# The prompt's down projection of a SwiGLU FFN as seven block products for eight, with the sample's part behind it

## The chip, the cores and the metric

The kernel runs on one core of a Trainium2 chip. The time is the device time of one execution in microseconds (us); three runs of the kernel before are at hand, and one more execution with a profile. Engines: TensorE (PE in the profile; its weight loads are PEld), VectorE (DVE), ScalarE (ACT), GpSimd (POOL) and SyncE (SP), which issues most of the transfers.

## The reference

One encoder layer and a final norm, applied to a prompt (1024 tokens) and a sample (256 tokens) with the same weights; D_MODEL is 1024 and D_FF 2816. The parts ahead of the FFN are left out here.

```python
    h = rmsnorm(x, norm_ffn_w)
    gu = h @ ffn_w_gate_up
    x = x + (jax.nn.silu(gu[..., :D_FF]) * gu[..., D_FF:]) @ ffn_w_down
    return x
...
        return rmsnorm(x, final_norm_w)
```

## The kernel before

Activations lie with channels on the 128 partitions and tokens along the free axis. Tokens are three blocks (`BLOCKS`): two of 512 for the prompt and one of 256 for the sample. D_FF is 22 tiles f of 128, D_MODEL 8 tiles m (or k) of 128. Matrices are fp32, and each operand is split into a rounded part and its remainder (`split`: ACT copies it to fp32r, L125; DVE or POOL subtracts, L126). `mm3` (L108) makes one product of three matmuls: hi by hi, hi by lo, lo by hi.

PE runs its instructions in the order in which the program writes them. The other engines are ordered by a tile scheduler, which works with estimates of durations and the dependences; each engine, and each queue of transfers, then runs its list strictly in order. Work to be done beside the main products (the norms) is written as side generators that yield a number of ns to wait for (`LAGS`, `LAGF`, `PACEF`), and `K.main` puts their PE instructions between the products when they are due by its own clock.

The up projection (`ff_first` for f = 0, `ff_up` for f = 1 to 21) already makes the prompt's gate and up of one f by seven block products for eight. Its outputs per f are the gated values of the prompt's two blocks and of the sample. Before, they go to DRAM as they are (`gd`, one row per f; `times_up`).

The down projection (`ffn_down`, `down`) reads them back. It goes over eight groups of f (`DOWN`: 2, 2, then six of 3). Within a group it goes over 8 m and 3 blocks; a PSUM bank sums a group's f, and DVE adds 0.5 times the bank to the residual in SBUF (L1717). So 192 banks are read. Weights of a group (`in_w_dn`, one tile of 128 x 1024 per f) are split on ACT and DVE, the gated values (`g_load`, 128 x 1280) on ACT and POOL or DVE. In the last group a `Norm` per block adds up squares as each m is done (`nm.add`, by POOL for the first `FADD[b]` of them, else DVE). Its rest (`Norm.rest`) sums them over partitions on PE (`nacc`), takes a reciprocal root on DVE (`nst`, ten small operations, L224 to L228), spreads it over partitions on PE, and scales and stores the output. The sample's norm is the last of all, behind the last product.

In front of the up projection stands the norm of the third block's FFN input. It is a side generator with the lag `LAGS`, so its PE instructions fall between products of the first f. Four banks hold raw operands (`r2_raw`) there, until L1535 has read them.

Of the kernel before, what the change touches and what calls it, by code (L numbers as in the profile page):

```python
# [8 lines left out]
F32 = mybir.dt.float32  # L9
# [20 lines left out]
DOWN = ((0, 1), (2, 3)) + tuple((f, f + 1, f + 2) for f in range(4, NFF, 3))  # L30
# [133 lines left out]
def trunk_kernel(ctx: ExitStack, tc: tile.TileContext, a):  # L164
# [1236 lines left out]
    gd = dp.tile([NFF, P, NTOK], F32, name="gd")  # L1401
# [136 lines left out]
    def make_room():  # L1538
        nonlocal room, c22
        room = x0p.tile([P, KT, 512], F32, tag="x0", name="room")  # L1540
        c22 = room[:, 7, :]

    fp = room = c22 = None
# [8 lines left out]
    def copied(ps, t=None):  # L1552
        if t is None:
            turns["p"] += 1
            t = room[:, 4 + turns["p"] % 3, :]
# [16 lines left out]
    def gate_of(ps, p, g=None):  # L1572
        g = ff(x2p, "nacc", "g", bufs=2) if g is None else g
        V.tensor_tensor(out=g, in0=p, in1=ps, op=ALU.add)  # L1574
        return silu2(g)

    def times_up(t, u, f, t0, n, sign):
        V.scalar_tensor_tensor(out=t, in0=u, scalar=sign, in1=t, op0=ALU.mult, op1=ALU.mult)
        SY.dma_start(gd[f, :, t0 : t0 + n], t)

    K.lo_vector = True
    K.order += [(a["w_dn"][g], "fp" if g > 1 and g % 3 else "wp") for g in range(NFF)]
    g_of = {}

    def g_load(i):

        if i == len(DOWN):
            return
        gh, gl = (hp.tile([P, 3, NTOK], F32R, tag=f"{x}{i % 2}", name=f"g{x}") for x in ("hi", "lo"))
        g_of[i] = []  # L1590
        for j, f in enumerate(DOWN[i]):
            for sl in (slice(0, 640), slice(640, NTOK)) if i == 0 else (slice(0, NTOK),):
                raw = K.raw()[:, :640] if i == 0 else fp.tile([P, NTOK], F32, tag="graw", name="graw", bufs=3)
                SY.dma_start(raw, gd[f, :, sl])
                split(gh[:, j, sl], gl[:, j, sl], raw, V if j % 2 else G)
            g_of[i].append((gh[:, j, :], gl[:, j, :]))
# [7 lines left out]
    def ff_first():  # L1604
# [19 lines left out]
        t2 = gate_of(pf, u2, u2)  # L1624
# [12 lines left out]
        u3 = copied(pa, cs[:, 2, :])  # L1637
        V.tensor_tensor(out=u3, in0=u3, in1=pe, op=ALU.add)
        times_up(t2, u3, 0, 512, 512, -1.0)
        yield from gu_mm(pa, w(3), 1, t4, False)  # L1640
        times_up(t1, pa, 0, 0, 512, -1.0)

    def ff_up(f):
# [198 lines left out]
```

## Time and profile before

| | us |
|---|---|
| median of three runs (lowest, highest) | 2325.65 (2325.51, 2326.88) |
| the profiled execution, its own time | 2328.12 |
| its span, first to last instruction | 2326.3 |

| | |
|---|---|
| mean granted clock | 0.989 |
| first down product starts | 1995.54 us |
| last down product starts | 2310.83 us |

A page gives the busy time per engine, the span in 40 slices with tenths of busy time, the granted clock in tenths and GB/s, the queues, the chain that ended last, the costliest groups and the transfers with the time from issue to landing. Rows of the trace give start, duration, engine, line, operation, output and inputs by the program's names, partitions by elements, and in brackets the idle time ahead of it and what ended that.

### The profile page before, as it was taken

To read this page: it belongs to the slowest core of one execution; us is meant where nothing else is said; L and a number is where in the kernel's file an instruction comes from. 1 tells how busy PE (TensorE), PEld (TensorE's weight loads), DVE (VectorE), ACT (ScalarE), POOL (GpSimd) and SP (SyncE) were. 2 spreads that over 40 slices of the span, in tenths; PEclk is the share of its full clock that TensorE was granted. 3 is DMA by queue.
4 is the path that set the end of the run, shared out by engine and by line. 5 is a ranking of instruction groups with operands and counts; after the bars stand their busy time and mean duration, and the time that the engine had idled before them with its cause. 6 is when DMAs were issued, how large, how long until landed. Compare 5 with 4: busy or idle time off the path is not lost.

```text
span 2326.3 us, 32511 instructions
## 1 busy us (share of the span) xinstructions
PE 2241.6 (96%) x12596; PEld 1947.7 (84%) x12596; DVE 1313.0 (56%) x2759; ACT 754.1 (32%) x1387; POOL 567.6 (24%) x362
## 2 busy tenths in 40 slices
PE   6999999999999999999999998999999999999997
PEld 6988888888888888888888886888888888888886
DVE  7758687887976955554543557323223223656445
ACT  5433242333423433132344523322322322312113
POOL 3010000000000000021322420766566565212113
PEclk9999999999999999999999999999999999999998
DMA  5221412323243537861223422211211211723202
GB/s 182 87 86 50 116 49 84 83 59 91 71 122 107 181 104 242 261 209 68 91 87 108 160 73 73 86 62 64 73 62 64 91 62 52 260 87 112 73 10 91
DMA packets 170453, 237.84 MB, mean 102 GB/s; under 512 B 71530, under 2 KB 99002, under 8 KB 170298
## 3 DMA queue, kind: packets, MB, share of 16 engines
q1 hardware_dynamic: 150458, 206.65, 28.0%
q10 hardware_dynamic: 19840, 29.11, 3.4%
q8 instruction: 99, 1.62, 0.3%
q14 instruction: 56, 0.46, 0.1%
HBM read 166.20 MB, written 69.51 MB: 101 GB/s over the span
## 4 chain that ended last, share of the span: by engine, by line
PE 46%; DVE 2%; DMA 1%; issue 1%; POOL 1%; ACT 0%; POOLq 0%; ACTq 0%; DVEq 0%; SPq 0%
PE bank L108 45%; DMA raw<-in_w_dn 0%; DMA kraw<-vd 0%; PE bank L121 0%; POOL x L272 0%; POOL wlo L126 0%; DVE wlo L126 0%; POOL kv L126 0%; DMA kraw<-kd 0%; DMA raw<-in_w_gu 0%; DVE x L1717 0%; DMA raw<-gd 0%; DVE t4l L126 0%; DVE x L1526 0%; DVE r2l L126 0%
## 5 line engine op out<-in xcount | busy, mean ns | idle before, releaser
L108 PE MATMUL bank<-hi,whi 128*128 128x512 f32 (+1 forms) x2144 | 766.5, 358 | 0.9 <-ACT whi L125 0.9
L108 PE MATMUL bank<-hi,wlo 128*128 128x512 f32 (+1 forms) x2144 | 751.1, 350 | 2.9 <-POOL wlo L126 1.8
L108 PE MATMUL bank<-lo,whi 128*128 128x512 f32 (+1 forms) x2144 | 751.4, 350 | 0.4 <-POOL lo L126 0.4
L108 PEld LDWEIGHTS bank<-hi,wlo 128*128 128x128 f32 x2144 | 407.2, 190 | 58.1 <-POOL wlo L126 2.2
L108 PEld LDWEIGHTS bank<-hi,whi 128*128 128x128 f32 x2144 | 408.1, 190 | 51.2 <-ACT whi L125 1.4
L108 PEld LDWEIGHTS bank<-lo,whi 128*128 128x128 f32 x2144 | 408.2, 190 | 49.9 <-POOL lo L126 0.7
L126 POOL TENSOR_TENSOR wlo<-raw,whi 128x1024 fp32r<-128x1024 f32 x71 | 180.5, 2545 | 439.1 <-ACT whi L125 435.9
L125 ACT ACTIVATE whi<-raw 128x1024 fp32r<-128x1024 f32 x151 | 159.4, 1060 | 355.5 <-PE bank L108 281.5
L108 PE MATMUL bank<-ghi,whi 128*128 128x512 f32 (+1 forms) x528 | 189.3, 358 | 1.3 <-DVE x L1717 1.3
L108 PE MATMUL bank<-ghi,wlo 128*128 128x512 f32 (+1 forms) x528 | 188.3, 357 | 0.5 <-DVE wlo L126 0.5
L108 PE MATMUL bank<-glo,whi 128*128 128x512 f32 (+1 forms) x528 | 187.3, 355 | 0.0
L1717 DVE SCALAR_TENSOR_TENSOR x<-bank,x 128x512 f32<-128x512 f32 (+1 forms) x192 | 112.4, 598 | 125.3 <-PE bank L108 120.0
L126 POOL TENSOR_TENSOR wlo<-room,whi 128x1024 fp32r<-128x1024 f32 x42 | 100.8, 2400 | 129.5 <-ACT whi L125 129.5
L126 DVE TENSOR_TENSOR wlo<-raw,whi 128x1024 fp32r<-128x1024 f32 x80 | 106.6, 1338 | 31.0 <-ACT whi L125 30.9
L108 PEld LDWEIGHTS bank<-ghi,whi 128*128 128x128 f32 x528 | 99.3, 188 | 17.2 <-DVE x L1717 2.2
L108 PEld LDWEIGHTS bank<-ghi,wlo 128*128 128x128 f32 x528 | 99.2, 188 | 16.4 <-DVE wlo L126 1.0
L108 PEld LDWEIGHTS bank<-glo,whi 128*128 128x128 f32 x528 | 99.4, 188 | 15.1
L126 POOL TENSOR_TENSOR glo<-graw,ghi 128x1280 fp32r<-128x1280 f32 x13 | 46.3, 3576 | 203.7 <-ACT ghi L125 203.7
L1680 DVE TENSOR_TENSOR room<-room,bank 128x512 f32<-128x512 f32 x21 | 14.4, 687 | 143.2 <-ACT room L1556 143.2
L125 ACT ACTIVATE whi<-room 128x1024 fp32r<-128x1024 f32 x42 | 44.5, 1061 | 143.4 <-PE bank L108 143.4
L1574 DVE TENSOR_TENSOR g<-room,bank 128x512 f32<-128x512 f32 x42 | 28.9, 688 | 103.4 <-PE bank L108 103.4
L591 DVE SCALAR_TENSOR_TENSOR acc<-craw,sm,acc 128x510 f32<-128x510 f32 (+1 forms) x96 | 72.5, 756 | 25.4 <-ACT acc L589 24.3
(302 smaller groups left out, 3803.2 us busy)
## 6 DMA issues: line engine op xcount, KB each, us to landing
raw<-in_w_gu SPq DMA_DIRECT2D x44, 512.0 KB, 3.9
graw<-gd SPq DMA_DIRECT2D x20, 640.0 KB, 5.5
gd<-t SPq DMA_DIRECT2D x44, 256.0 KB, 2.5
raw<-in_w_dn SPq DMA_DIRECT2D x22, 512.0 KB, 4.3
raw<-in_w_g SPq DMA_DIRECT2D x20, 512.0 KB, 3.5
gtd<-gs ACTq DMA_DIRECT2D x32, 256.0 KB, 2.0
raw<-in_w_qkv SPq DMA_DIRECT2D x12, 512.0 KB, 3.6
x<-in_xT SPq DMA_DIRECT2D x10, 512.0 KB, 5.7
```

The source lines that it names most:

```text
L108: self.nc.tensor.matmul(out, l, r, start=start, stop=stop, skip_group_check=more)
L125: self.nc.scalar.activation(hi, src, AF.Copy)
L126: (eng or self.nc.vector).tensor_tensor(out=lo, in0=src, in1=f32(hi), op=ALU.subtract)
L591: V.scalar_tensor_tensor(out=dst, in0=src, scalar=wj, in1=dst, op0=ALU.mult, op1=ALU.add)
L1574: V.tensor_tensor(out=g, in0=p, in1=ps, op=ALU.add)
L1680: V.tensor_tensor(out=c22, in0=u3, in1=pe, op=ALU.add)
L1717: V.scalar_tensor_tensor(out=x2[b][:, m, :], in0=ps, scalar=0.5, in1=x2[b][:, m, :], op0=ALU.mult, op1=ALU.add)
```

## The change

The prompt's down projection is written as seven block products over pairs of f: a pair (even f, odd f) by the two halves of D_MODEL is one side, by the two blocks of tokens the other. The second operand (B) is combined in `combine` as the gated values are made, and seven versions are stored for each of 11 pairs (`gq`); the sample's go to `gsd`. The first operand (A, weights) is combined on DVE in `a_prep`. A phase is one of the seven products: 11 pairs by 4 tiles of 128 output channels, summed in four banks ("a" or "b") over all pairs; "b" and "a" are kept over several phases, and 28 evictions of 512 wide take the place of 128. Within a phase, weights come in units of one or two pairs (`a_split` into a ring of three) and B in bundles of 3, 4 and 4 pairs (`b_load`, `b_split`). The first units and bundles are loaded in the last f of the up projection (`down_early`). The sample's part (`down_sample`) follows, with f one after the other, and 8 evictions. The norm of block 1 starts after the sixth phase, that of block 0 after the seventh, that of the sample at the end. `nm.add` for the prompt is on POOL, for the sample on DVE. `LAGS` and the second `LAGF` grow.

```diff
-DOWN = ((0, 1), (2, 3)) + tuple((f, f + 1, f + 2) for f in range(4, NFF, 3))
+PAIRS = NFF // 2
...
-    gd = dp.tile([NFF, P, NTOK], F32, name="gd")
+    gq = dp.tile([7, PAIRS, P, 512], F32, name="gq")
+    gsd = dp.tile([NFF, P, NS], F32, name="gsd")
...
+    def combine(f, t1, t2):
+        p = f // 2
+        if f % 2 == 0:
+            r = ff(x2p, "nacc", "r", bufs=2)
+            V.tensor_tensor(out=r, in0=t1, in1=t2, op=ALU.subtract)
+            SY.dma_start(gq[2, p], r)
+            pending["r"], pending["b12"] = r, t2
             return
+        r, b12 = pending["r"], pending["b12"]
+        V.scalar_tensor_tensor(out=r, in0=r, scalar=-1.0, in1=t2, op0=ALU.mult, op1=ALU.subtract)
+        SY.dma_start(gq[3, p], r)
+        V.tensor_tensor(out=b12, in0=t2, in1=b12, op=ALU.subtract)
+        SY.dma_start(gq[4, p], b12)
+        t4_ = ff(x2p, "nsq", "t", bufs=3) if f == NFF - 1 else t1
+        V.scalar_tensor_tensor(out=t4_, in0=r, scalar=-1.0, in1=t1, op0=ALU.mult, op1=ALU.subtract)
+        SY.dma_start(gq[6, p], t4_)
+    def store1(f):
+        return gq[f % 2, f // 2]
+    def store2(f):
+        return gq[5, f // 2] if f % 2 else None
...
+    units = [slice(0, 1)] + [slice(i, i + 2) for i in range(1, PAIRS, 2)]
+    bundles = [slice(0, 3), slice(3, 7), slice(7, PAIRS)]
+    unit_of = {p: i for i, u in enumerate(units) for p in range(u.start, u.stop)}
+    bundle_of = {p: i for i, u in enumerate(bundles) for p in range(u.start, u.stop)}
+    w_dn = a["w_dn"].rearrange("(k e) p m -> e p k m", e=2)
...
+    def b_load(j):
+        if j >= 7 * len(bundles):
+            return
+        ph, i = divmod(j, len(bundles))
+        ps = bundles[i]
+        n = ps.stop - ps.start
+        if j == 0:
+            raw = x2p.tile([P, 4, 512], F32, tag="x2", name="braw")
+        else:
+            raw = hp.tile([P, 4, 512], F32, tag="lo2" if j % 2 and j > 1 else "hi2", name="braw")
+        SY.dma_start(raw[:, :n, :], gq[ph, ps].rearrange("k p t -> p k t"))
+        b_raw[j] = raw
+    def b_split(j):
+        if j >= 7 * len(bundles):
+            return
+        ps = bundles[j % len(bundles)]
+        t = hp.tile([P, 2, 4, 512], F32R, tag="lo0" if j % 2 else "hi0", name="bhl")
+        n = ps.stop - ps.start
+        raw = b_raw.pop(j)
+        for x in ([0, 1] if n == 3 else [0, 2]):
+            sl = slice(x, x + 1 if n == 3 and x == 0 else x + 2)
+            split(t[:, 0, sl, :], t[:, 1, sl, :], raw[:, sl, :], V)
+        b_hl[j] = t
+    def a_room(i):
+        if i % 3 < 2:
+            return tuple(t.rearrange("p (k c) -> p k c", c=512) for t in pair_of(wp))
+        t = down_room()
+        return t[:, 0], t[:, 1]
+    def a_split(i, src):
+        n = src.shape[1]
+        a_hl[i] = tuple(t[:, :n, :] for t in a_room(i))
+        split(*a_hl[i], src, V)
...
+    def down_early(step):
+        if step == 0:
+            b_load(0)
+            early_raw(1, K.raw()[:, :1024].rearrange("p (k c) -> p k c", c=512))
+            pair_home(0)
+            SY.dma_start(home[0][0][0], w_dn[0][:, units[0], :])
+            b_split(0)
+            a_split(0, part(0, 0, 0))
+        elif step == 1:
+            b_load(1)
+            t = hp.tile([P, 4, 512], F32, tag="lo2", name="araw")
+            early_raw(2, t[:, 0:2, :])
+            early_raw(3, t[:, 2:4, :])
+        else:
+            a_split(1, early[1])
+            b_split(1)
+            b_load(2)
...
+            combine(*pending["last"])
...
+    def down_room():
+        return dpool.tile([P, 2, 2, 512], F32R, tag="x2", name="ahl")
...
+    def a_prep(i):
+        ph, u = divmod(i, len(units))
...
+        if ph == 0:
+            src = early[u] if u in early else p(0, 0)
+        elif ph == 1:
+            src = p(1, 0)
+        elif ph == 2:
+            src = p(0, 1)
+            V.tensor_tensor(out=src, in0=src, in1=p(1, 1), op=ALU.add)
...
+        else:
+            src = p(1, 1)
+        a_split(i, src)
+    STEPS = (("a", 0, 0, 0, 1), ("b", 0, 0, 0, 1), ("b", 0, 1, 1, -1), ("a", 1, 0, 1, 1), ("a", 1, 1, 1, -1), ("b", 1, 0, 1, 1), ("a", 1, 1, 0, -1))
...
+    def down_prompt():
+        a_prep(2)
+        norms = {}
+        for b in (1, 0):
+            norms[b] = Norm(x2p, 512)
+        sums = {}
+        for ph, (key, more, half, b, sign) in enumerate(STEPS):
+            if not more:
+                sums[key] = [bank(pm if key == "a" else pq) for _ in range(4)]
+            ps = sums[key]
+            def product(m, p, start, stop):
+                i = len(units) * ph + unit_of[p]
+                j = len(bundles) * ph + bundle_of[p]
+                k, q = p - units[unit_of[p]].start, p - bundles[bundle_of[p]].start
+                t = b_hl[j]
+                x = [(*(w[:, k, m * P : (m + 1) * P] for w in a_hl[i]), t[:, 0, q, :], t[:, 1, q, :])]
+                yield from mm3(ps[m], x, start and not more, stop, bool(more))
+            final = (half, b) in ((0, 0), (1, 1), (0, 1), (1, 0)) and ph in (1, 4, 5, 6)
+            def evac(m):
+                x = x2[b][:, 4 * half + m, :]
+                V.scalar_tensor_tensor(out=x, in0=ps[m], scalar=0.5 * sign, in1=x, op0=ALU.mult, op1=ALU.add)
+                if final:
+                    norms[b].add(x, G)
+            for u, pairs in enumerate(units):
+                i = len(units) * ph + u
+                pairs = range(pairs.start, pairs.stop)
+                if u < len(units) - 1:
+                    for p in pairs:
+                        for m in range(4):
+                            yield from product(m, p, p == 0, False)
+                else:
+                    for m in range(4):
+                        for p in pairs:
+                            yield from product(m, p, False, p == PAIRS - 1)
+                        evac(m)
+                for load in loads.get(i, ()):
+                    load[0](*load[1:])
+                if i == 1:
+                    pair_home(1)
+                    SY.dma_start(home[1][0][0], w_dn[1][:, units[0], :])
+                a_prep(i + 3)
+                if pairs[-1] + 1 == bundles[bundle_of[pairs[-1]]].stop:
+                    j = len(bundles) * ph + bundle_of[pairs[-1]]
+                    b_split(j + 2)
+                    if j == 0:
+                        b_load(3)
+                    b_load(j + 4)
+                if ph == 6:
+                    sample_loads(u)
+            if ph == 5:
+                last_norm(norms[1], 1)
+        last_norm(norms[0], 0)
...
+    order_s = [2 * p + 1 for p in range(PAIRS)] + [2 * p for p in range(PAIRS)]
+    g_s = {}
+    def g_room(i, tag, n):
+        t = hp.tile([P, 2, n, NS], F32R, tag=tag, name="gs")
+        for k in range(i, min(i + n, NFF), 2):
+            raw = x2p.tile([P, 512], F32, tag="nsq", name="graw", bufs=3).rearrange("p (k t) -> p k t", k=2)
+            for x in range(2):
+                SY.dma_start(raw[:, x, :], gsd[order_s[k + x]])
...
+    def down_sample():
+        for us in ((0,), (1, 2), (3, 4), (5,)):
+            w_load(0, 0, us)
+        g_room(16, "hi0", 6)
+        nm = Norm(x2p, NS)
+        his, los = ([t[:, 512 * k : 512 * k + 512] for t in (w0, w1) for k in range(2)] for w0, w1 in zip(pair_of(wp), pair_of(wp)))
+        def prep(n):
+            if n < 2 * NFF:
+                half, i = divmod(n, NFF)
+                e, p = (1, i) if i < PAIRS else (0, i - PAIRS)
+                t, k = home[e][unit_of[p]]
+                k += p - units[unit_of[p]].start
+                split(his[n % 4], los[n % 4], t[:, k, 512 * half : 512 * half + 512], V)
+        for n in range(4):
+            prep(n)
+        for half in range(2):
+            ps = [bank(pm)[:, :NS] for _ in range(4)]
+            def product(m, i):
+                n = NFF * half + i
+                sl = slice(m * P, (m + 1) * P)
+                yield from mm3(ps[m], [(his[n % 4][:, sl], los[n % 4][:, sl], *g_s[i])], i == 0, i == NFF - 1)
+            for i in range(NFF - 2):
+                for m in range(4):
+                    yield from product(m, i)
+                prep(NFF * half + i + 4)
+                if half == 0 and i == 2:
+                    for us in ((0,), (1, 2), (3, 4), (5,)):
+                        w_load(0, 1, us)
+            for m in range(4):
+                for i in range(NFF - 2, NFF):
+                    yield from product(m, i)
+                x = x2[2][:, 4 * half + m, :]
+                V.scalar_tensor_tensor(out=x, in0=ps[m], scalar=0.5, in1=x, op0=ALU.mult, op1=ALU.add)
+                nm.add(x, V)
+            for i in range(NFF - 2, NFF):
+                prep(NFF * half + i + 4)
+        last_norm(nm, 2)
...
-            nm = Norm(x2p, n)
-            for m in range(KT):
-                yield from down(g_of[i], ws, m, b)
-                nm.add(x2[b][:, m, :], G if m < FADD[b] else V)
...
-LAGS, FIRST_W = 13500, 9000
+LAGS, FIRST_W = 19000, 9000
-LAG0, LAGF, PACEF = 7500, (3500, 2800, 1500), 500
-FADD = (6, 4, 0)
+LAG0, LAGF, PACEF = 7500, (3500, 3500, 1500), 500
```

PE in the first f of the up projection: `hi`, `lo`, `hi1`, `lo1` are the parts of the activations, `whi`, `wlo` those of a weight, `cst` by `nacc` is the norm's sum over partitions. Before:

```order
L108 MATMUL bank_13393<-hi1_12890,wlo_13379 128x512 [waits DVE_49]
L108 MATMUL bank_13393<-hi1_12890,whi_13378 128x512 [waits Activation_49]
L108 MATMUL bank_13393<-lo1_12891,whi_13378 128x512
L108 MATMUL bank_13393<-hi1_12890,wlo_13379 128x512
L108 MATMUL bank_13459<-cst_74,nacc_12587 128x1 [waits DVE_49,PE_49]
L108 MATMUL bank_13459<-cst_74,nacc_12587 128x1
L108 MATMUL bank_13393<-hi1_12890,whi_13378 128x512 [waits Activation_49]
L108 MATMUL bank_13393<-lo1_12891,whi_13378 128x512
L108 MATMUL bank_13393<-hi1_12890,wlo_13379 128x512
L108 MATMUL bank_13393<-hi1_12890,whi_13378 128x512 [waits Activation_49]
```

After:

```order
L108 MATMUL bank_13509<-hi0_12889,whi_13465 128x512
L108 MATMUL bank_13509<-lo0_12890,whi_13465 128x512
L108 MATMUL bank_13509<-hi0_12889,wlo_13466 128x512
L108 MATMUL bank_13509<-hi0_12889,whi_13465 128x512
L108 MATMUL bank_13509<-lo0_12890,whi_13465 128x512
L108 MATMUL bank_13509<-hi0_12889,wlo_13466 128x512
L108 MATMUL bank_13519<-cst_74,nacc_12588 128x1 [waits DVE_49,PE_49]
L108 MATMUL bank_13519<-cst_74,nacc_12588 128x1
L108 MATMUL bank_13509<-hi0_12889,whi_13465 128x512
L108 MATMUL bank_13509<-lo0_12890,whi_13465 128x512
L108 MATMUL bank_13509<-hi0_12889,wlo_13466 128x512
```

The norm's sum stood inside the product of the third weight, behind one that reads tile `hi1`; it stands inside a later-written product of `hi0` now, with the bank of `r2_raw` no longer next.

ACT where the up projection ends and the down projection begins: `bhl` is a split bundle, `ahl` and `whi` a split unit, `braw` and `araw` what was loaded for them. Before:

```order
L125 ACTIVATE whi_17484<-raw_17482 128x1024 [waits DMAHW4_49,Pool_49]
L1556 ACTIVATE room_13526<-bank_17313 128x512 [waits PE_49,Activation_49]
L125 ACTIVATE whi_17490<-raw_17488 128x1024 [waits DMAHW5_49,Pool_49]
L1568 ACTIVATE t_17508<-g_17506 128x512 [waits DMAHW1_49,DVE_49]
L125 ACTIVATE whi_17558<-raw_17532 128x1024 [waits DMAHW6_49,PE_49]
L125 ACTIVATE ghi_17568<-graw_17570 128x1280 [waits DMAHW1_49,PE_49]
L125 ACTIVATE ghi_17568<-graw_17574 128x1280 [waits DMAHW2_49]
L125 ACTIVATE whi_17772<-raw_17746 128x1024 [waits DVE_49,DMAHW3_49,Activation_49,Pool_49]
L125 ACTIVATE whi_17564<-raw_17562 128x1024 [waits DMAHW7_49,PE_49]
```

After:

```order
L1557 ACTIVATE room_13508<-bank_17352 128x512 [waits DMAHW0_49,PE_49]
L1569 ACTIVATE t_17549<-room_13508 128x512 [waits DMAHW6_49,DVE_49]
L125 ACTIVATE bhl_17529<-braw_17506 128x1024 [waits DMAHW4_49]
L125 ACTIVATE bhl_17529<-braw_17506 128x1024
L125 ACTIVATE whi_17602<-araw_17508 128x1024 [waits DMAHW5_49,PE_49,Activation_49]
L125 ACTIVATE bhl_17638<-braw_17534 128x1024 [waits DMAHW0_49,PE_49]
L125 ACTIVATE bhl_17638<-braw_17534 128x1024
L125 ACTIVATE ahl_17581<-araw_17508 128x1024 [waits DMAHW4_49,DMAHW3_49,DMAHW6_49,DMAHW2_49,DVE_49]
L125 ACTIVATE whi_17634<-w0_17573 128x1024 [waits DMAHW6_49,Activation_49]
L125 ACTIVATE ahl_17673<-w0_17575 128x1024 [waits DMAHW7_49,DVE_49,PE_49]
```

Splits of a weight and of gated values stood by turns; now the split of unit 2 (`ahl_17581`, of `araw_17508`) stands behind that of unit 3 (`whi_17602`) and that of the third bundle (`bhl_17638`), which waits for PE and for the transfer into `braw_17534`.

DVE in the norm of block 1: `nst` is its reciprocal root, `bank` a scratch row. Before:

```order
L227 TENSOR_TENSOR bank_19592<-bank_19592,nst_19597 128x4 [waits DVE_49]
L228 SCALAR_TENSOR_TENSOR nst_19597<-bank_19592,nst_19597 128x4 [waits DVE_49]
L226 SCALAR_TENSOR_TENSOR bank_19592<-nst_19597,bank_19592 128x4 [waits DVE_49]
L1717 SCALAR_TENSOR_TENSOR x1_17524<-bank_19588,x1_17524 128x512 [waits PE_49]
L227 TENSOR_TENSOR bank_19592<-bank_19592,nst_19597 128x4 [waits DVE_49]
L228 SCALAR_TENSOR_TENSOR nst_19597<-bank_19592,nst_19597 128x4 [waits DVE_49]
L226 SCALAR_TENSOR_TENSOR bank_19592<-nst_19597,bank_19592 128x4 [waits DVE_49]
L227 TENSOR_TENSOR bank_19592<-bank_19592,nst_19597 128x4 [waits DVE_49]
L228 SCALAR_TENSOR_TENSOR nst_19597<-bank_19592,nst_19597 128x4 [waits DVE_49]
L1717 SCALAR_TENSOR_TENSOR x1_17524<-bank_19619,x1_17524 128x512 [waits PE_49]
```

After:

```order
L228 SCALAR_TENSOR_TENSOR nst_18775<-bank_18770,nst_18775 128x4 [waits DVE_49]
L226 SCALAR_TENSOR_TENSOR bank_18770<-nst_18775,bank_18770 128x4 [waits DVE_49]
L227 TENSOR_TENSOR bank_18770<-bank_18770,nst_18775 128x4 [waits DVE_49]
L228 SCALAR_TENSOR_TENSOR nst_18775<-bank_18770,nst_18775 128x4 [waits DVE_49]
L226 SCALAR_TENSOR_TENSOR bank_18770<-nst_18775,bank_18770 128x4 [waits DVE_49]
L227 TENSOR_TENSOR bank_18770<-bank_18770,nst_18775 128x4 [waits DVE_49]
L126 TENSOR_TENSOR wlo_18811<-w1_17574,whi_18810 128x1024 [waits PE_49,Activation_49]
L228 SCALAR_TENSOR_TENSOR nst_18775<-bank_18770,nst_18775 128x4 [waits DVE_49]
L126 TENSOR_TENSOR bhl_18814<-braw_18667,bhl_18814 128x1024 [waits DMAHW6_49,Activation_49]
L126 TENSOR_TENSOR bhl_18814<-braw_18667,bhl_18814 128x1024 [waits Activation_49]
```

An eviction (L1717) stood between two steps of the chain; now the remainder of a weight (`wlo_18811`), which waits for PE and ACT, stands ahead of the last step.

More of the change, by code (lines that the diff above doesn't have):

```diff
@@ L1585, in g_load, with gate_of @@
-    def g_load(i):
-        if i == len(DOWN):
-            return
[L1589 to L1596, printed above, removed]
+    def gate_of(ps, p):
+        V.tensor_tensor(out=p, in0=p, in1=ps, op=ALU.add)
+        return silu2(p)
@@ L1741, in trunk_kernel @@
+    def ffn_down():
+        for load in loads.pop(0):
+            load[0](*load[1:])
+        yield from down_prompt()
+        yield from down_sample()
     K.main(ffn_down())
```

154 lines of the change are left out of this document (103 added, 51 removed).

## The prediction

> **What bounds the kernel now.** I read the page first (busy time, the slices), then stretches of the down projection, then its rows in order of time, then PE's waits there and where the prompt's first FFN tile begins.
>
> ```profile
> PE 2241.6 (96%) x12596; PEld 1947.7 (84%) x12596; DVE 1313.0 (56%) x2759; ACT 754.1 (32%) x1387; POOL 567.6 (24%) x362
> 1996.00:2311.00 315.00, 311.54 (x1615) 264.18 (x1613) 176.94 (x260) 64.04 (x74) 61.33 (x25) 1.00 0.28 98
> 1995.54 0.39 PE L108 MATMUL bank<-ghi,whi 128*128 128x512 f32 x1
> ...
> 2310.00 0.28 PE L108 MATMUL bank<-glo,whi 128*128 128x256 f32 x1
> ...
> 2310.83 0.28 PE L108 MATMUL bank<-ghi,wlo 128*128 128x256 f32 x1
> 2315.61 0.99 PE L108 MATMUL bank<-cst,nacc 128*128 128x1 f32 x4 [4.50 <-DVE nacc L244]
> ```
>
> The first row is the page, the second a stretch (its length, then the busy time of PE, weight loads, DVE, ACT and POOL, the granted clock, the DMA share, GB/s). PE bounds the whole and this stage: 311.5 of 315 us at clock 1.00. The stage runs from 1995.54 to 2311.05, 315.5 us; a tail follows that ends the span at 2326.3.
>
> Busy time of pipelined matmuls is modelled, so I take their price from starts. The last eight 256-wide starts are 0.83 us apart in all, 0.119 each. For the 512-wide ones I use two evictions of 256-wide blocks, one m apart (9 x 2 products of 512 and 9 of 256 between them):
>
> ```profile
> 2153.79 0.42 DVE L1717 SCALAR_TENSOR_TENSOR x<-bank,x 128x256 f32<-128x256 f32 x1 [0.38 <-PE bank L108]
> ...
> 2159.02 0.42 DVE L1717 SCALAR_TENSOR_TENSOR x<-bank,x 128x256 f32<-128x256 f32 x1 [0.38 <-PE bank L108]
> ```
>
> 5.23 - 9 x 0.119 = 4.16, over 18: **0.231 us** a 512-wide product. The stage's 1056 x 0.231 + 528 x 0.119 = 306.8; 8.7 us of its 315.5 are something else.
>
> **The change part by part.**
>
> *Products.* Prompt: 8 tiles of m x 22 f x 2 blocks x 3 = 1056 before, 7 x 11 pairs x 4 tiles x 3 = 924 now. 132 x 0.231 = **-30.5 us**. The new operands' rows aren't in this trace; the matmuls of the row at 1443.35 and on, at half clock, are the dearest seen, and the nearest are these, so I bound the term by a tenth on either side, -27 to -33. The sample keeps 528 x 0.119 = 62.8.
>
> *Lost waits.* The norms of blocks 0 and 1 stand inside the stage already, as four groups of products, and stay:
>
> ```profile
> 2284.98 0.95 PE L108 MATMUL bank<-cst,nacc 128*128 128x1 f32 x8
> ...
> 2308.16 1.16 PE L108 MATMUL bank<-cst,nst 128*128 128x128 f32 x8 [1.58 <-DVE nst L228]
> ...
> PE bank L108 <- DVE x L1717: 1.3, 1, 1.3
> PE bank L108 <- DVE wlo L126: 0.5, 1, 0.5
> ```
>
> About 1.05 each by these two, 4.2 of the 8.7. The other 4.5 are waits that this order of work has: the 1.58 for nst, 1.3 for an eviction, 0.5 for a weight remainder (the last two rows are PE's waits in this stage), and 1.1 in gaps too small for a row. All go with their code, **-4.5** (bounds 0, if others as long take their place, and -4.5); those that I can place are added below.
>
> *A wait at the start.* PE's fourth pair needs the split of unit 2. In ACT's order that split stands behind the split of B's third bundle, whose load SP issues only when the second bundle has been split out of the same buffer. These rows are the nearest:
>
> ```profile
> graw<-gd SPq DMA_DIRECT2D x20, 640.0 KB, 5.5
> oraw<-od SPq DMA_DIRECT2D x2, 1280.0 KB, 7.5
> 1988.29 1.06 ACT L125 ACTIVATE whi<-raw 128x1024 fp32r<-128x1024 f32 x1 [3.07 <-DMA raw<-in_w_dn]
> 1991.59 1.22 DVE L126 TENSOR_TENSOR wlo<-raw,whi 128x1024 fp32r<-128x1024 f32 x1 [0.39 <-ACT whi L125]
> ```
>
> A bundle of 1 MB lies between the two transfers: an estimate of 6.7 us. Counted from the first down product: the second bundle's load is issued about 3 us before it (SP waits for the sample's last product of the up stage, 24 products earlier, and for a store behind it), so it lands at 3.7; two ACT splits, a DVE remainder and handovers, 7.2; the third bundle's load, 13.9; three ACT splits at 1.06, 17.2. PE comes there after 36 products, 8.3. That is 8.9 us of wait, and 0.9 for the remainder behind it (1.22 + 0.16 - 2 products). Then PE may run at half clock for a while:
>
> ```profile
> 1442.51 0.98 PE L108 MATMUL bank<-cst,nacc 128*128 128x1 f32 x4 [6.70 <-DVE x L1535]
> 1443.35 0.77 PE L108 MATMUL bank<-hi,whi 128*128 128x512 f32 x1
> ...
> 1447.27 0.39 PE L108 MATMUL bank<-r2h,whi 128*128 128x512 f32 x1
> 1454.96 0.80 PE L108 MATMUL bank<-hi,wlo 128*128 128x512 f32 x1 [1.78 <-POOL wlo L126]
> ...
> 1460.99 0.40 PE L108 MATMUL bank<-lo,whi 128*128 128x512 f32 x1
> ```
>
> After the 6.7 us wait nine products took 3.92 us where 2.08 would do, 1.8 lost; after 1.78 us fourteen took 6.03 for 3.23, 2.8 lost. I take 2.0: **+11.8 us**. Bounds: 4 (loads land as early as the 512 KB rows do, full clock) and 17 (each load 2 us later, 2.8).
>
> *Norms on the way.* Block 1's norm runs inside the last of the seven products, block 0's in the sample's part. Before, its chain of small DVE operations stood among evictions; now a weight remainder stands in it that waits for PE to finish a unit, since it reuses that unit's buffer, and PE's statistics product stands right behind that unit and waits for the chain. So PE idles for 1.06 (ACT) + 1.22 (DVE) + 0.16 and two handovers, **+2.7**. In the sample the same happens with two 512-wide splits and a bundle's remainder ahead: **+3.6**. Behind the waiting statistics product all of PE's products are queued, and behind the remainder the rest of the chain. Bounds of both together: 0 (the buffer is free early) to 12. The upper one has half clock: behind the 1.78 us at 1454.96 PE lost 2.8, which twice makes 5.6 and 2306.0 for the whole; behind the 1.58 us at 2308.16 its next products (from 2310.00) start at the full pace. I add nothing. The Trainium skill (TensorE: Matmul & The Clock Gate, Part 1: The HAM clock gate) lets the clock halve only after an idle window of about 3.4 us, which would leave both norm waits at full clock. The row at 2308.16 agrees with that, the one at 1454.96 does not.
>
> *Tail.* Before, the tail waits 4.5 us for the last square's sum over eight tiles; now the last block is the sample's own 256 wide, whose sums run while PE works, and four last evictions remain. These are the last of each before:
>
> ```profile
> 2312.30 0.42 DVE L1717 SCALAR_TENSOR_TENSOR x<-bank,x 128x256 f32<-128x256 f32 x1
> ...
> 2312.86 0.42 ACT L243 ACTIVATE nsq<-x 128x256 f32<-128x256 f32 x1 [0.62 <-DVE x L1717]
> ...
> 2314.64 0.82 DVE L244 TENSOR_TENSOR nacc<-nacc,nsq 128x256 f32<-128x256 f32 x1
> ```
>
> Evictions and sums shared DVE with the output of block 1 (two operations of L276 stood between). Without that, 0.42 + 0.42 + 0.82 = 1.66 follow the last product in place of 4.5: **-2.9** (bounds 0 and -4.5). The rest of the tail is the same.
>
> *First FFN tile.* The sample's norm is started later (LAGS). Before, PE's norm product there waited for a bank of the set that is held until L1535 reads it, and went to half clock:
>
> ```profile
> PE bank L108 <- DVE x L1535: 6.7, 1, 6.7
> PE bank L108 <- DVE nst L228: 1.3, 1, 1.3
> 1400.00:1500.00 100.00, 86.12 (x476) 73.91 (x476) 59.40 (x115) 34.70 (x59) 35.94 (x23) 0.91 0.22 74
> ```
>
> Now it stands some products later, after the bank is free. The 6.7 us and 1.8 of half clock go, 3 us come back at its second product (the row of nst before: 1.3, with more in front): **-5.5** (bounds 0 and -10; a rival could also leave PE waiting for t4's operands, 1.8 for wlo).
>
> *Nothing.* The sums on the way up (four DVE operations of 512 and four stores per pair of f) and the operands' work in the down stage lie beside PE:
>
> ```profile
> DVE  7758687887976955554543557323223223656445
> ...
> GB/s 182 87 86 50 116 49 84 83 59 91 71 122 107 181 104 242 261 209 68 91 87 108 160 73 73 86 62 64 73 62 64 91 62 52 260 87 112 73 10 91
> L1717 DVE SCALAR_TENSOR_TENSOR x<-bank,x 128x512 f32<-128x512 f32 x97 | 66.4, 689 | 102.2 <-PE bank L108 102.2
> L126 DVE TENSOR_TENSOR wlo<-raw,whi 128x1024 fp32r<-128x1024 f32 x15 | 25.1, 1703 | 1.6 <-ACT whi L125 1.6
> L126 POOL TENSOR_TENSOR glo<-graw,ghi 128x1280 fp32r<-128x1280 f32 x10 | 36.2, 3641 | 163.0 <-ACT ghi L125 163.0
> ```
>
> In the slices of the up stage (58 us each, the nine that read 3 2 3 2 2 3 2 2 3) DVE is busy two to three tenths, so 4 x 0.69 = 2.8 us per pair fit; without that cover they would cost 11 x 2.8 = 30. In a phase of the down stage (one of the seven products) DVE makes 11 remainders of 1024 (1.22 each by the row at 1991.59), in four phases 5.5 sums of that width, which I put at the same, and 4 to 8 evictions at 0.69: at most 13.4 + 6.7 + 5.5 = 25.6 us, beside 132 x 0.231 = 30.5 of PE. Without the cover see the third rival. Loads are 7 x 11 x 0.26 = 20 MB of B, 11.5 MB of weights about twice and 5 MB of x2, 48 MB in 290 us or 165 GB/s, where a slice has shown 260.
>
> *Sum.* -30.5 - 4.5 + 11.8 + 2.7 + 3.6 - 2.9 - 5.5 = -25.3. The durations are from an execution of 2328.12 us (span 2326.3 and 1.8 around it), 2.5 above the median of the runs, 2325.65; less 25.3 from the profiled one is 2302.8, from the median **2300.4**, which I give.
>
> **The rivals.**
>
> *The loads are in time.* If the second bundle lands before the down stage starts, the chain ahead of unit 2 ends about 4 us late: 2292.6; with the norm waits at 0 as well, 2286. For it: a 512 KB load from DRAM took 4.3 us. Against it: the third load's buffer must be free first.
>
> *Later loads.* Two stalls instead of one, as the weights' 2 MB loads of the first phases go through the same queue as the bundles (issued by SP in order, and x2's behind them), or the first FFN tile gives nothing: +6 to +20, 2306 to 2320, at its centre 2314. For it: slices of 260 GB/s with several transfers open.
>
> *DVE becomes the bound*, which ends slower. Its remainder takes 1.22 us alone but 1.70 in the middle of the stage (the row of 15), where POOL subtracts as well. In the four phases with sums DVE has 16.5 operations of that width and, at most, 5.5 us of evictions, so it decides above (30.5 - 5.5) / 16.5 = 1.52. At 1.70 a phase takes 33.6, and four such are 12 us more, 2313; at 1.9, 25.5 us more, the saving is gone; at 2.2, 2346. The Trainium skill (SBUF — State Buffer, its rule on the shared port pair) explains such a rise by a lock that a DVE operation with two SBUF inputs and one of GpSimd hold in turns; by it the rise goes where POOL is idle. The rows of 1.22 and 1.70 agree. In the new stage only the sums of squares remain on POOL, so I give this little.
>
> *The saving isn't on the path* (the change doesn't do what it says): if a wait of 4 us comes at each of the six later phases too, for the loads behind the buffers of A and B, 24 us come back: 2324, between 2321 and 2330. Against it: a phase's first unit is split while PE still works on two others, some 5 us each.
>
> **How the numbers follow.** Forecast, 2293 to 2308: 0.50. Loads in time, 2285 to 2293: 0.22. Later loads, 2308 to 2321: 0.18. No change, 2321 to 2330: 0.05. DVE the bound, above 2330: 0.05. The range takes the forecast, the earlier case and the nearer half of the later one: 2285 to 2313, which leaves out 0.10 of late cases above, 0.05 of the others, and some 0.05 below. A measurement of this kernel tells 0.2% (4.7 us) from no change. Faster by more than that: 0.92, within: 0.03, slower: 0.05.
>
> **What would show it.** In the profile after: the down stage is 924 products of 512; a wait of PE for ACT or DVE of about 10 us near the eighth microsecond of the down stage, with half clock behind it; two waits for nst of 2 to 4 us; the nacc wait of the tail below 2; the wait for L1535 gone; DVE's 1024-wide remainder near 1.22 us. The prediction is wrong if that remainder is above 1.4 over a whole phase, if PE waits at each phase's start, or if the products' cadence rises above 0.235.

## The result and the profile after

The changed kernel takes 2304.36 us (median of four, 2299.72 to 2305.49), the kernel before on the same chip 2325.58 (2322.76 to 2326.88): a ratio of 0.9907, 95% interval 0.9889 to 0.9924, or about 21 us less. 2300.4 was predicted. The profiled executions are 2328.12 us and 2304.28, their spans 2326.3 and 2301.6, 24.7 apart; most of what follows is counted in spans.

The busy times on the page after:

```profile
PE 2214.0 (96%) x12464; PEld 1929.4 (84%) x12464; DVE 1389.9 (60%) x2773; ACT 815.9 (35%) x1480; POOL 531.9 (23%) x353
```

The stretch from the first down product to the last (columns as for the kernel before):

```profile
1988.80:2289.30 300.50, 284.10 (x1485) 244.72 (x1483) 192.91 (x235) 127.16 (x170) 32.31 (x21) 0.97 0.48 165
```

PE's waits from the last f of the up projection to the end (total, times, longest):

```profile
PE bank L108 <- ACT ahl L125: 9.6, 1, 9.6
PE bank L108 <- DVE nst L228: 8.1, 3, 3.5
PE bank L108 <- DVE nacc L244: 1.6, 1, 1.6
PE bank L108 <- POOL nacc L244: 1.0, 1, 1.0
```

132 instructions are gone from PE, as forecast. The stage took 315 us, of which PE was idle 3.5; it takes 300.5, of which PE is idle 16, and the granted clock falls from 1.00 to 0.97. So part of the gain was turned into waits: one of 9.6 us for a weight operand, two for norm chains (the 8.1 less 2.3 us that belong to the tail) and one of 1.0 us for a sum of squares.

Span against span, by the first rows of each part:

| part | before | after | difference |
|---|---|---|---|
| start to the first `nacc` x8 of the prompt's second FFN norm | 1407.76 | 1407.60 | -0.2 |
| from there to the first `t4` product (first FFN tile) | 59.44 | 54.56 | -4.9 |
| rest of the up projection | 528.34 | 526.64 | -1.7 |
| first to last down product | 315.29 | 300.42 | -14.9 |
| last product to the end | 15.5 | 12.4 | -3.1 |

The chain that makes the first wait. ACT's time line: unit 3's split, bundle 3's, unit 2's.

```profile
1994.54 1.04 ACT L125 ACTIVATE whi<-araw 128x1024 fp32r<-128x1024 f32 x1
2002.65 2.00 ACT L125 ACTIVATE bhl<-braw 128x1024 fp32r<-128x1024 f32 x2 [7.07 <-DMA braw<-gq]
2005.57 1.06 ACT L125 ACTIVATE ahl<-araw 128x1024 fp32r<-128x1024 f32 x1 [0.91 <-DMA gq<-t]
```

SP's time line: the issues of bundle 3's load and of the last store of the last pair's sums.

```profile
1996.11 0.36 SPq L1633 DMA_DIRECT2D braw<-gq  x1
...
1998.44 0.59 SPq L1604 DMA_DIRECT2D gq<-t  x1
```

PE's time line: the 24 products of unit 2, the bracket with the idle time ahead of them, and the next ones.

```profile
2006.68 7.66 PE L108 MATMUL bank<-bhl,ahl 128*128 128x512 f32 x24 [9.56 <-ACT ahl L125]
2014.18 0.61 PE L108 MATMUL bank<-bhl,whi 128*128 128x512 f32 x2
```

Two things are to be seen. Bundle 3's load lands 6.5 us after its issue (forecast 6.7), and its split does stand ahead of unit 2's. But behind that split ACT waits 0.91 us more, until a store of the last sums (`gq<-t`) has landed, 7 us after its issue. And the 24 products that follow take 7.50 us by their starts where 24 of the later phases take 5.46: 2.0 of half clock, as forecast.

The norm of block 1 in PE's time line:

```profile
2186.62 1.05 PE L108 MATMUL bank<-cst,nacc 128*128 128x1 f32 x8 [1.02 <-POOL nacc L244]
2187.53 0.98 PE L108 MATMUL bank<-bhl,whi 128*128 128x512 f32 x2
...
2195.05 1.16 PE L108 MATMUL bank<-cst,nst 128*128 128x128 f32 x8 [2.25 <-DVE nst L228]
```

The end of its chain in DVE's:

```profile
2191.43 0.17 DVE L227 TENSOR_TENSOR bank<-bank,nst 128x4 f32<-128x4 f32 x1
2193.70 1.22 DVE L126 TENSOR_TENSOR wlo<-w,whi 128x1024 fp32r<-128x1024 f32 x1 [2.10 <-ACT whi L125]
2194.84 0.15 DVE L228 SCALAR_TENSOR_TENSOR nst<-bank,nst 128x4 f32<-128x4 f32 x1
```

DVE idles 2.10 us ahead of a weight remainder, with one step of the norm's chain behind it, and PE idles for that step: the wait that the order showed. The wait of 1.02 us for POOL's sum of squares wasn't forecast. Behind it and the eight narrow products of the norm (0.91 us) PE goes to half clock: two products from 2187.53 to 2188.32, 0.79 in place of 0.46, and so on until 2190.88. In two of the runs below the same wait stands there and no half clock follows, so this is what happened in this execution and not what the wait always costs.

### The profile page after: what moved, and what is told of

It reads as the page before. It is cut to its first block, busy times and chain, and to the rows that moved or that the text cites. A ratio compares the mean times of both kernels' runs of the same rounds, so it can differ in the third digit from the quotient of the medians.

```text
span 2301.6 us, 32403 instructions
## 1 busy us (share of the span) xinstructions
PE 2214.0 (96%) x12464; PEld 1929.4 (84%) x12464; DVE 1389.9 (60%) x2773; ACT 815.9 (35%) x1480; POOL 531.9 (23%) x353
## 4 chain that ended last, share of the span: by engine, by line
PE 42%; issue 4%; DVE 2%; DMA 1%; POOL 1%; ACT 1%; POOLq 0%; SPq 0%; ACTq 0%; DVEq 0%
PE bank L108 42%; DMA kraw<-vd 0%; DMA braw<-gq 0%; POOL nacc L244 0%; PE bank L121 0%; DMA gq<-t 0%; DVE wlo L126 0%; POOL kv L126 0%; DMA kraw<-kd 0%; DMA raw<-in_w_dn 0%; POOL x L272 0%; ACT whi L125 0%; ACT nsq L243 0%; DVE x L1528 0%; DVE t4l L126 0%
## 5 line engine op out<-in xcount | busy, mean ns | idle before, releaser
L125 ACT ACTIVATE whi<-raw 128x1024 fp32r<-128x1024 f32 (+1 forms) x141 | 144.5, 1025 | 213.9 <-PE bank L108 151.5
L108 PE MATMUL bank<-bhl,whi 128*128 128x512 f32 x392 | 121.9, 393 | 0.0
L126 DVE TENSOR_TENSOR wlo<-raw,whi 128x1024 fp32r<-128x1024 f32 (+1 forms) x70 | 79.9, 1142 | 50.2 <-ACT whi L125 50.1
L108 PE MATMUL bank<-bhl,ahl 128*128 128x512 f32 x336 | 81.3, 398 | 9.6 <-ACT ahl L125 9.6
L591 DVE SCALAR_TENSOR_TENSOR acc<-craw,sm,acc 128x510 f32<-128x510 f32 (+1 forms) x96 | 72.4, 755 | 24.7 <-ACT acc L589 23.5
L108 PEld LDWEIGHTS bank<-bhl,whi 128*128 128x128 f32 x392 | 74.2, 190 | 15.6
L108 PEld LDWEIGHTS bank<-bhl,ahl 128*128 128x128 f32 x336 | 63.9, 191 | 24.5 <-ACT ahl L125 10.0
L126 DVE TENSOR_TENSOR wlo<-w,whi 128x512 fp32r<-128x512 f32 (+1 forms) x59 | 52.4, 890 | 48.0 <-ACT whi L125 47.8
L737 DVE TENSOR_TENSOR W<-W,UT 128x2 f32<-128x2 f32 (+30 forms) x155 | 73.1, 472 | 13.2 <-DMA W<-in_eye 8.6
L243 ACT ACTIVATE nsq<-x 128x512 f32<-128x512 f32 (+1 forms) x70 | 40.4, 584 | 107.4 <-DVE x L1227 93.5
L108 PE MATMUL bank<-bhl,wlo 128*128 128x512 f32 x196 | 76.9, 392 | 0.0
```

What stands on the lines that cost most here:

```text
L108: self.nc.tensor.matmul(out, l, r, start=start, stop=stop, skip_group_check=more)
L125: self.nc.scalar.activation(hi, src, AF.Copy)
L126: (eng or self.nc.vector).tensor_tensor(out=lo, in0=src, in1=f32(hi), op=ALU.subtract)
L243: S.activation(sq, x, AF.Square)
L591: V.scalar_tensor_tensor(out=dst, in0=src, scalar=wj, in1=dst, op0=ALU.mult, op1=ALU.add)
L737: V.tensor_tensor(out=t3, in0=u3[:, i:, c:].rearrange("p j c -> p c j"), in1=XL[:, 32 * i + i : 32 * i + 32].unsqueeze(1).to_broadcast([P, ...
```

## The experiments

Executions of one kernel differ by up to 8 us (2317.49 to 2325.20 in one of them). Much of that can lie ahead of the FFN: the first `nacc` x8 above comes at 1402 to 1408 us in the twelve traces. So a part is judged by its own length in the trace, beside the medians. The ratios are to the kernel before on the same chip, whose median was 2324.5 to 2325.6 us each time.

**Unit 2 or its room?** The first run changes the place of unit 2's split in ACT's order and leaves its room as it is; the second gives it other room, and the third does so for two more units.

```diff
+        elif step == 2:
+            a_split(1, early[1])
         else:
-            a_split(1, early[1])
             b_split(1)
             b_load(2)
...
             combine(f, t1, c22)
+            down_early(3)
```

> The last pair's sums (combine) are written ahead of the split of the second bundle; in ACT's order the split of unit 2 (ahl) now stands ahead of that of the third bundle, and its room is where it was. Theory O (the prediction's: unit 2 is late because it stands behind the third bundle's split on ACT): the 9.6 us wait of PE for ahl falls below 1 and the half clock behind it goes, 2304.4 - 11 = about 2293. Theory M (unit 2's room is memory in which the last sums of the up stage stood, and it is free only when their stores to DRAM have landed, about 7 us after issue): the sums end about 1.2 us earlier, so the wait falls only to about 8, time about 2303.

Measured: 2296.22 us (2292.63 to 2297.30), ratio 0.9874 (0.9860 to 0.9889), down stage 296.7 us from first to last product. ACT's time line in this run:

```profile
1990.35 1.04 ACT L125 ACTIVATE whi<-araw 128x1024 fp32r<-128x1024 f32 x1
1995.78 1.06 ACT L125 ACTIVATE ahl<-araw 128x1024 fp32r<-128x1024 f32 x1 [4.38 <-DMA gq<-t]
2000.79 2.00 ACT L125 ACTIVATE bhl<-braw 128x1024 fp32r<-128x1024 f32 x2 [3.96 <-DMA braw<-gq]
```

Unit 2's split now stands ahead of the third bundle's, and ACT still waits 4.38 us for the store of the last sums; PE waits 4.1. PE's wait fell from 9.6 to 4.1 where theory O expected less than 1, so the order alone doesn't set it. Theory M holds in kind, and its size was off: the store lands 3.2 us after its issue rather than 7, with no bundle's load ahead of it in the queue.

```diff
+    ahl2 = hp.tile([P, 2, 2, 512], F32R, tag="hi1", name="ahl")
...
+        if i == 2:
+            return ahl2[:, 0], ahl2[:, 1]
```

(The home of the weights of units 1 and 2, in the same room, is made when they are loaded.)

> Unit 2's split goes to room that the last product of the up stage frees (tag hi1), no longer where the last sums stood. Theory O and theory M: PE's wait for ahl goes. What then? Theory W (a wait behind it was covered): PE gets to unit 4 at about 16.3 us of the stage, and its weights land only at about 20.7, since their room too waits for the stores of the last sums; a wait of 4 to 6 us comes there, time about 2298. Theory N (nothing behind it): the whole 9.6 and the 2 of half clock go, about 2293.

Measured: 2295.77 us (2292.69 to 2297.12), ratio 0.9873 (0.9859 to 0.9888), down stage 293.9. The split in ACT's time line, which now comes ahead of both bundles' (1993.42 and 2003.05):

```profile
1989.29 1.06 ACT L125 ACTIVATE ahl<-araw 128x1024 fp32r<-128x1024 f32 x1 [7.81 <-PE bank L108]
```

PE's waits:

```profile
PE bank L108 <- DVE nst L228: 8.2, 3, 3.6
PE bank L108 <- ACT whi L125: 3.7, 1, 3.7
```

The wait for `ahl` is gone. With other room the split also got the first place in ACT's order, so this run takes away both causes at once and doesn't tell what the old place would cost with free room. A wait of 3.7 us for unit 4's weights is there, as theory W has it (4 to 6 expected). Those weights are loaded into room that the last sums' stores hold too: SP waits 2.7 us for a store (`gq<-room`) before it issues their load.

```diff
-        0: [(w_load, 0, 0, (4,)), (w_load, 0, 0, (5,))],
+        0: [(raw_load, 4, 0), (raw_load, 5, 2)],
...
-        8: [(w_load, 0, 0, (1, 2)), (w_load, 0, 0, (3,))],
+        8: [(w_load, 0, 0, (1, 2)), (w_load, 0, 0, (3, 4)), (w_load, 0, 0, (5,))],
...
+    def raw_load(u, k):
+        early_raw(u, f1[0][:, k : k + 2, 512:])
```

> As the kernel before it, and the first phase's weights of units 4 and 5 are loaded into room that no store holds (1 MB more is loaded in the second phase). Theory W: those weights land before PE wants them, the wait that moved to unit 4 goes too, at most 1.5 us is left (the third bundle's remainder), time about 2294. Rival (the transfers of the first phase, 339 GB/s with a 0.96 share, are the limit): the wait turns up again at another load within the first two phases, and the time stays near 2298.

Measured: 2286.80 us (2285.18 to 2289.63), ratio 0.9839 (0.9822 to 0.9855), down stage 289.4, 11.0 less than the changed kernel. No wait of PE is left in the first two phases, so the transfers weren't the limit, though 1 MB more was loaded. The total is better than forecast in part because this run's `nacc` x8 came at 1402.

**The norms' chains.**

```diff
-            yield 2800
+            yield gap
             pb = bank()
...
+GAPF = (8000, 8000, 2800)
```

> In the two prompt norms PE's second product is written 8000 ns, not 2800 ns, behind the first by the program's clock. Theory (DVE's chain is held up by weight remainders, and PE stands right behind it): the waits for nst of 2.3 and 3.5 us go, and the half clock behind the second one (about 3 us with the slow norm products), -8 to -9, about 2296. Rival (the scheduler spreads the chain over the longer gap, and PE waits as before): 2304.

Measured: 2290.06 us (2288.59 to 2291.52), ratio 0.9851 (0.9836 to 0.9865). The down stage is 292.0, 8.4 less, inside the theory's 8 to 9. Of the three waits for `nst` the tail's 2.3 is left. The scheduler did not stretch the chain into the new gap.

**The first FFN tile.**

```diff
-LAGS, FIRST_W = 19000, 9000
+LAGS, FIRST_W = 13500, 9000
```

> The changed kernel with LAGS back at 13500, nothing else. Theory (the first FFN tile became shorter through the place of the norm's products alone): from the first product of the prompt's second norm (nacc x8) to the first product of t4, 54.6 us now, 59.4 us before, goes back to 59.4, with PE's wait of 6.7 us for L1535; down stage 300.4 as it is. Rival (the other changes in the first tile, the sums kept in place, made it shorter): 54.6 stays.

The same constant alone, in the kernel before:

> The kernel before with LAGS 19000, nothing else. Theory: the same stretch falls from 59.4 to about 54.6, the down stage stays at 315.3, so about 5 us less than before, 2320.5. Rival: 59.4 stays, 2325.5.

Measured, from `nacc` x8 to the first `t4`: 59.55 us with 13500 in the changed kernel, 54.54 with 19000 in the kernel before (54.56 and 59.44 without these edits). In the first of them PE's waits have this row again:

```profile
PE bank L108 <- DVE x L1537: 6.7, 1, 6.7
```

So LAGS alone makes the first tile 4.9 us shorter, and nothing else of the change does. The totals show it less well: LAGS alone gives 2322.18 us of ten (2317.49 to 2325.20), ratio 0.9988 (0.9978 to 0.9997), 2.5 less than the 2324.71 before; put back it gives 2302.97 (2299.98 to 2304.18), which the spread of the part ahead can't tell from 2304.36.

**DVE's cover.** Some DVE work is done more than once.

```diff
         split(*a_hl[i], src, V)
+        V.tensor_tensor(out=a_hl[i][1], in0=src, in1=f32(a_hl[i][0]), op=ALU.subtract)
...
-            V.tensor_tensor(out=r, in0=t1, in1=t2, op=ALU.subtract)
+            for _ in range(4):
+                V.tensor_tensor(out=r, in0=t1, in1=t2, op=ALU.subtract)
```

> The changed kernel with DVE work done more than once: each remainder of a weight operand twice (11 x 0.6 = 6.7 us a phase, 47 us over the seven), and the first sum of each pair on the way up four times (11 x 3 x 0.69 = 23 us). Cover theory (both lie beside PE): the up stage from the first t4 to the first down product stays at 526.6 within 0.5; the down stage grows by 0 to 8 from 300.4, as only the third phase (DVE busy 29.9 of 30.6 us) has no room. Rival (DVE on the path): up 549, down 330 or more.

One execution: 2312.04 us. The up stage takes 526.65 us, the same to 0.01, with 23 us of work added; the down stage 308.05, 7.6 more, with 47 us asked for (DVE busy 230.6 us there, before 192.9). PE's waits tell where most of the 7.6 are:

```profile
PE bank L108 <- DVE nst L228: 14.3, 3, 8.5
PE bank L108 <- ACT ahl L125: 8.7, 1, 8.7
PE bank L108 <- DVE nacc L244: 1.6, 1, 1.6
PE bank L108 <- DVE ahl L1660: 1.3, 1, 1.3
PE bank L108 <- DVE x L1899: 0.7, 1, 0.7
```

6.2 us more than in the changed kernel are for the norms' chains, which stand in DVE's queue behind the added work, 1.3 for an operand and 0.7 for an eviction; the waits for ACT and POOL are 0.9 and 0.8 shorter. So DVE is hardly on the path of the products; it is on that of the chains.

**All of it together.** First with the first tile's second norm at a gap of 7000 as well (edits of the third and fourth run, block 1 at LAGF 6000, and `gap=7000` where LAGS is used).

> Units 2, 4 and 5 in other room, the norms' second products 8000 ns behind the first, block 1's norm at LAGF 6000, and 7000 ns in the first FFN tile's second norm (its nst wait of 4.5 and half clock behind it). If the waits add: down stage 315.3 - 34 = about 280 (289.4 of the run with units moved, less 8.4 of the norm gap, less 1 to 2 of the nacc wait), first tile 54.6 - 6 = 48.5; time about 2286.8 - 9.5 - 6 = 2271. Rival (they hide one another, or a load comes next): 2280.

Measured: 2280.70 us (2278.62 to 2281.25), ratio 0.9806 (0.9791 to 0.9820), down stage 277.4: the waits there add. The first tile is 46.2 us, 8.3 less, and the rest of the up stage 536.7, 10 more. There the rival is right: PE now meets the same norm (3.1 us) and a remainder by POOL (2.4 us) behind `t4`, with half clock after them. Without that part:

> As the run with all waits taken out, without the change in the first FFN tile: units 2, 4 and 5 in other room, the prompt norms' second products 8000 ns behind the first, block 1's norm at LAGF 6000. If the down stage's waits add without the first tile: down stage 277.4, first tile 54.6 and up stage 526.6 as in the changed kernel; that is 1.7 us shorter than the run with the first tile's gap (which had 46.2 and 536.7), about 2279. Rival (its gain in the first tile was real): 2283.

Measured: **2276.85 us** of five (2275.61 to 2279.75), ratio 0.9797 (0.9783 to 0.9810). The stretch of the whole down stage:

```profile
1985.00:2262.50 277.50, 277.42 (x1485) 240.38 (x1484) 190.81 (x235) 126.74 (x169) 31.07 (x21) 1.00 0.52 183
```

PE is busy 277.42 of 277.50 us at clock 1.00. This version beats both kernels, and shows the price of all waits in the changed kernel's stage: 300.4 - 277.4 = 23.0 us.

**The price of a product.** In the changed kernel DVE's time line has the first eviction of two phases' ends, 132 products apart:

```profile
2117.34 0.69 DVE L1897 SCALAR_TENSOR_TENSOR x<-bank,x 128x512 f32<-128x512 f32 x1
...
2147.37 0.68 DVE L1897 SCALAR_TENSOR_TENSOR x<-bank,x 128x512 f32<-128x512 f32 x1
```

30.03 over 132 is 0.2275 us, not 0.231.

```diff
                     for p in pairs:
-                        for m in range(4):
+                        pass
+                    for m in range(4):
+                        for p in pairs:
                             yield from product(m, p, p == 0, False)
```

> The changed kernel with the units of two pairs in another order: for each tile of 128 outputs both pairs, six products in a row into one bank where it was three. It asks why a product took 0.2275 us (30.02 a phase of 132) and not the 0.231 of the kernel before, where nine in a row went into one bank. Theory L (a longer row into one bank costs more; the last unit of a phase, six in a row, has evictions 1.38 us apart, 0.230 a product): a phase takes 30.2 to 30.3. Rival (it's something else, the tiles' layout for example): 30.0.

One execution, 2297.95 us: the same two evictions stand at 2115.80 and 2145.82, 30.02 apart. Theory L falls as far as it was tried: six products in a row into one bank take what three take. Nine in a row weren't run in the new stage, and why the old products took 0.231 stays open.

This run shows another thing. It has the changed kernel's waits, and its down stage is 297.3 us, 3.2 shorter. The rows of the norms:

```profile
2185.07 1.05 PE L108 MATMUL bank<-cst,nacc 128*128 128x1 f32 x8 [1.02 <-POOL nacc L244]
2185.99 0.71 PE L108 MATMUL bank<-bhl,whi 128*128 128x512 f32 x2
2186.54 0.40 PE L108 MATMUL bank<-bhl,wlo 128*128 128x512 f32 x1
...
2226.69 1.16 PE L108 MATMUL bank<-cst,nst 128*128 128x128 f32 x8 [3.27 <-DVE nst L228]
```

Behind the same 1.02 us the two products take 0.55 us here, not 0.79, and behind 3.27 us the norm's products take 1.16 us, where they took 2.08 behind 3.54 in the changed kernel: no half clock in either place. (At the start it cost 1.1 us more than there, 8.63 us for the 24 products.)

## Why the prediction was right, point by point

- **Products**, forecast -30.5. At 0.2275 the 924 products take 210.2 us, the 1056 before took 244.0 at 0.231: -33.8. The mis-sized part is the price of the new products, which the prediction took from the old ones. The bounds (-27 to -33) just missed it.
- **Lost waits**, -4.5. By the best version nothing but products is left in the stage (210.2 + 62.8 + 4.2 for the norms is 277.2, measured 277.4), so 4.3 of the old 315.3 were waits and gaps. Right.
- **The wait at the start**, +11.8. Measured 9.7 by the starts of PE's products and 2.0 of half clock, 11.8. The size is right. Of the mechanism, "In ACT's order that split stands behind the split of B's third bundle" is true, and the loads behaved as estimated: the third bundle's split ends at 2004.65, so by these rows the order alone would make 8.65 of the 9.56 us. What the step left out is the room that unit 2's split writes. The store `gq<-t` held it 0.91 us longer, and it makes a wait by itself: moved ahead of the third bundle's, the split still waited for a store (first run). The runs don't show the order's part by itself, since with other room (second run) the place in the order went too. So the prediction had one of two causes that end 0.9 us apart, and that the size fits to a tenth is in part luck. The row of ACT's order names four transfer queues in the waits of that split, which could have pointed to it.
- **Norms on the way**, +2.7 and +3.6. The waits for `nst` were 2.3 and 3.5, as forecast. "I add nothing" for half clock was wrong for this execution: the two norms cost 23.0 - 11.8 = 11.2 in all: 5.8 of waits for `nst`, 1.0 for POOL, and the rest half clock, behind the 1.02 us and behind the 3.5. Weighing the rule, I kept the row at 2308.16 (full clock behind 1.58 us) and dropped the one at 1454.96 (half behind 1.78). This trace has half clock behind 1.02 us and none behind 2.25, so the length of one idle time does not decide. It is against the Trainium skill's rule (TensorE: Matmul & The Clock Gate, Part 1: The HAM clock gate) of an idle window of about 3.4 us; its 3.4 us until the clock is back agrees with 2187.5 to 2190.9. Nor does one kernel's wait decide: behind the same 1.02 us half clock came in four traces of six (this one, the first, third and fourth run) and not in the second and the last run. So the term was neither nothing nor fixed; it differs from one execution to the next, by some 4 us here.
- **Tail**, -2.9: -3.1 measured, with 1.65 for `nacc` against 1.66 forecast.
- **First FFN tile**, -5.5: -4.9, by LAGS alone (fifth and sixth run).
- **Nothing**, 0. The up stage even became 1.7 us shorter: 1.1 between the t4 products of the first tile and those of the second, where a wait of 0.4 for a remainder by POOL is gone, and 0.4 ahead of the last tile's t4 products, where one of 0.3 for ACT is gone. No run was made to find out why. DVE's cover held, with 193 us busy of 300, and 23 us of added work on the way up made that stage no longer. The third rival, DVE as the bound, didn't come. What it rests on was seen in one place: while POOL added squares, two of DVE's remainders took 4.20 us (2183.45), and elsewhere 2.36. This is in line with the lock of the Trainium skill (SBUF — State Buffer, its rule on the shared port pair).
- **The sum** was -25.3 and the spans differ by 24.7. Two errors cancel there, which is luck: the products gained 3.3 more than forecast and the norms cost 4.9 more. The medians differ by 21.2, and 2304.36 is 4.0 above the forecast: 2.5 because the forecast was taken off the median before and the execution profiled before was that much longer, 0.6 in the sum, and 0.9 in time outside the span (1.8 before, 2.7 after).

The time of the rival "The loads are in time" is what the third run reached by giving the operands room early, 2286.8; it was put at 2285 to 2293.

## What to carry to other kernels

A saving in products is worth its price only as far as the operands are there: 23 us of waits stood against 34 us of products here, and moving three tiles and two constants got them back. Where a queue's order and the wait list of one instruction both explain a wait, look at which tile's room it writes and who still holds it; here the room of a tile on its way to DRAM came free only when the store had landed, 3.2 to 7 us after its issue. The order can follow from the room: with free room the split came first. Chains of small operations on an engine with long work in its queue need distance on PE's side; move the consumer, not the chain.

## What the runs showed of the hardware that wasn't expected

- Half clock followed idle times of PE of 1.02 and 3.5 us, and none followed 2.25 us, in one trace. The same place differs between executions: behind 1.02 us it came in four traces of six, and behind 2.25 us in two of five (the first and third run, where the norm's eight products took 1.89 and 1.95 us in place of 1.16). By the granted clock its stretches in the changed kernel's down stage were 10.2, 3.4 and 6.8 us long, multiples of one length (from 2000.1, 2187.8 and 2228.7). What starts one wasn't tested.
- A product of the same shape took 0.231 us in the old down stage and 0.2275 in the new, constant over hundreds of products, at a granted clock of 1.00 in both. Six products in a row into one bank took what three took.
- The same instructions ahead of the FFN ended at 1402 to 1408 us from one execution to the next, in kernels that differ only behind that point.
